# A gate on GpSimd's first casting DMAs, moved from x row tile 0 to x row tile 3, in a fused matmul, GELU, matmul kernel

## The chip, the cores and the metric

The kernel runs on one core of a Trainium2 chip. The metric is the device time of one execution in microseconds (us). A kernel's number is the median of several executions, and it is compared with runs of the kernel before made on the same chip in the same session. Sessions fell on different chips, so each has its own runs of the kernel before. Matmul and weight load are called PE and PEld in the profile, VectorE is DVE, ScalarE is ACT, GpSimd is POOL, SyncE is SP.

## The reference

```python
batch, m, k, h, n = 16, 512, 768, 3072, 768      # all fp32

def reference(x, w1, b1, w2):
    y = np.matmul(x, w1) + b1
    y = 0.5 * y * (1.0 + erf(y / np.sqrt(2.0)))
    return np.matmul(y, w2).astype(np.float32)
```

## The kernel before

The kernel computes in f16 and handles x in blocks of 1024 rows. Both matmuls are done by Strassen-like sums. Only the first few microseconds matter here. Two ways of loading stand side by side in them: SyncE's plain DMAs bring four x row tiles (128 rows each) and the first block of w1 as fp32, which VectorE casts; GpSimd's DMAs bring everything else and cast on the way.

```python
        for t in range(4):                                   # x row tiles 0 to 3, fp32
            nc.sync.dma_start(out=xf[:, t, :], in_=xr[:, t, :])
        wts[0] = slots[0]
        for half in range(2):                                # w1 block 0, two halves, fp32
            r = slice(half * KQ, (half + 1) * KQ)
            nc.sync.dma_start(out=wf[:, r, :], in_=w1r[:, r, 0:2 * P])
        # ... bias, zeros, identities ...
        nc.gpsimd.tensor_copy(out=xh_of(0, 4)[:, 0:1], in_=xf[:, 0, 0:1])   # the gate
        load_wt(1)                                           # casting DMA: w1 block 1
        for t in range(4, 8):
            load_x(0, t)                                     # casting DMAs: x row tiles 4 to 7
        for n in range(2, 4):
            load_wt(n)
        # ...
        spin(9)                                              # matmuls on zeros
        for t in range(4):
            xhs[t] = xh_of(0, t)
            nc.vector.tensor_copy(out=xhs[t], in_=xf[:, t, :])
            transpose_pe(0, t, copy_halves if t == 3 else nc.scalar.copy)
            # ...
            spin(2)
        # ... VectorE casts w1 block 0; matmuls of block 0 on the top rows ...
        plain(1, 0, 0, 0)                                    # w1 block 1 is needed here
        transpose_pe(0, 4)                                   # x row tile 4
        plain(1, 0, 0, 1)
        plain_done(1, 0, 0)
        transpose_pe(0, 5, nc.vector.tensor_copy)
        plain(1, 0, 1, 0)
        transpose_pe(0, 6)
        # ...
```

The gate copies one element of each of 128 rows. Its result is overwritten by the DMA of tile 4. It is there only because GpSimd runs in order: all its DMAs wait until the element that is read has landed.

Of the kernel before, what the change touches and what calls it, by code (L numbers as in the profile page):

```python
# [22 lines left out]
def kernel(  # L23
# [8 lines left out]
    nc = tc.nc  # L32
# [56 lines left out]
    def cut(off, n, pattern=None, **dims):  # L89
        ap = arena[:, off:off + n]  # L90
        return ap.rearrange(pattern, **dims) if pattern else ap
# [113 lines left out]
    with tc.manual_schedule():  # L205
# [27 lines left out]
        def load_wt(n):  # L233
            hi = hi_of(n)
            if n >= NH:
                sb, k = divmod(n, NH)
                wts[n] = wt_far[k - 4] if 4 <= k < 7 else wt_late[(sb + 2 + k - 7 * (k > 6)) % 4]
                nc.sync.dma_start(out=wts[n], in_=w1s[hi][:])
                return
            wts[n] = slots[n]  # L240
            nc.gpsimd.dma_start(out=w1_raw(wts[n]), in_=w1r[:, :, 2 * hi * P:2 * (hi + 1) * P])
# [70 lines left out]
        def xh_of(sb, t):  # L312
            if sb < ONE:
                return cut(sb * GR + GR // 2 + t * K, K)
            return xh_mid[t % 5 if t < 5 else t - 5] if sb == ONE else xh_late[t % 3]
# [423 lines left out]
        xf = cut(GR, 8 * K).bitcast(FP32).rearrange("p (t k) -> p t k", t=4)  # L739
# [13 lines left out]
        nc.scalar.activation(out=zero[:, 1, 0:1], in_=zero[:, 0, 0:1], func=GELU)  # L753
        make_identity(nc, ident[:])
        make_identity(nc, idf)
        nc.gpsimd.tensor_copy(out=xh_of(0, 4)[:, 0:1], in_=xf[:, 0, 0:1])
        load_wt(1)
        for t in range(4, 8):
            load_x(0, t)
# [420 lines left out]
```

## Time and profile before

| | |
|---|---|
| median of three runs | 851.17 us (851.04 to 851.5) |
| span of the profiled run | 848.7 us |
| TensorE busy | 843.3 us, 99% |
| first real matmul | 9.39 us |
| w1 block 1, x tiles 4, 5, 6 and 7 land | 11.65, 12.60, 13.57, 14.53 and 15.46 us |

The rows that carry the argument are in the prediction. One thing to know for reading them: a DMA row of GpSimd is the time that it spends on issuing the DMA (called descriptor writing here); the data moves later, on q0 (issued at 4.57, first packet at 8.60). The landing is taken from the view of each issue, which gives the time from issue to landing.

### The profile page before, as it was taken

To read this page: it belongs to the slowest core of one execution; us is meant where nothing else is said; L and a number is where in the kernel's file an instruction comes from. 1 tells how busy PE (TensorE), PEld (TensorE's weight loads), DVE (VectorE), ACT (ScalarE), POOL (GpSimd) and SP (SyncE) were. 2 spreads that over 40 slices of the span, in tenths; PEclk is the share of its full clock that TensorE was granted. 3 is DMA by queue.
4 is the path that set the end of the run, shared out by engine and by line. 5 is a ranking of instruction groups with operands and counts; after the bars stand their busy time and mean duration, and the time that the engine had idled before them with its cause. 6 is when DMAs were issued, how large, how long until landed. Compare 5 with 4: busy or idle time off the path is not lost.

```text
span 848.7 us, 16767 instructions
## 1 busy us (share of the span) xinstructions
PE 843.3 (99%) x6546; PEld 577.6 (68%) x6546; DVE 673.5 (79%) x1134; ACT 426.4 (50%) x700; POOL 94.9 (11%) x151
## 2 busy tenths in 40 slices
PE   9999999999999999999999999999999999999998
PEld 5444445796544897449964499545995469964798
DVE  5766679777857997679967799668996699957997
ACT  4777763231287413773247721587116761277611
POOL 5021100042200002000020000200002100010000
PEclk9999999999999999999999999999999999999999
DMA  9998796699998699987999489994999949984397
GB/s 228 216 274 166 166 221 232 233 201 221 361 329 206 207 341 370 255 201 259 335 368 300 118 296 346 359 276 123 319 356 335 281 114 324 369 300 168 106 308 282
DMA packets 144819, 222.11 MB, mean 262 GB/s; under 512 B 61964, under 2 KB 85444, under 8 KB 144740
## 3 DMA queue, kind: packets, MB, share of 16 engines
q1 hardware_dynamic: 117392, 178.85, 66.4%
q0 software_dynamic: 27168, 42.08, 22.4%
q8 instruction: 51, 0.84, 0.4%
q14 instruction: 28, 0.23, 0.1%
q10 hardware_dynamic: 180, 0.11, 0.0%
HBM read 181.78 MB, written 49.45 MB: 272 GB/s over the span
## 4 chain that ended last, share of the span: by engine, by line
PE 99%; DMA 1%; SPq 0%; DVE 0%; ACT 0%; issue 0%
PE bY L416 22%; PE bY L520 15%; PE bX L416 14%; PE bX L520 10%; PE bZ L416 7%; PE bW L416 7%; PE bZ L520 5%; PE bW L520 5%; PE bY L459 4%; PE bZ L459 2%; PE bW L459 2%; PE bY L608 2%; PE bX L608 1%; PE bX L459 1%; DMA arena<-in_x_dram 1%; PE bZ L608 1%
## 5 line engine op out<-in xcount | busy, mean ns | idle before, releaser
L210 DVE TENSOR_TENSOR arena<-arena 128x1536 f16<-128x1536 f16 (+6 forms) x638 | 409.8, 674 | 4.8 <-DMA arena<-arena 0.7
L416 PEld LDWEIGHTS <-arena 128*128 128x128 f16 x2016 | 196.6, 98 | 220.1 <-issue 0.5
L520 PEld LDWEIGHTS <-arena 128*128 128x128 f16 x3528 | 292.1, 98 | 8.2
L416 PE MATMUL bY<-arena 128*128 128x512 f16 (+1 forms) x864 | 214.5, 375 | 0.0
L639 DVE TENSOR_TENSOR arena<-bY,arena 128x512 f32<-128x512 f32 (+1 forms) x102 | 69.4, 680 | 118.2 <-PE bY L416 88.3
L632 ACT COPY bY<-bX 128x512 f32<-128x512 f32 (+1 forms) x145 | 79.6, 549 | 118.1 <-DVE arena L569 87.8
L520 PE MATMUL bY<-arena 128*128 128x192 f16 x1500 | 138.3, 246 | 0.0
L416 PE MATMUL bX<-arena 128*128 128x512 f16 (+1 forms) x576 | 138.3, 375 | 0.0
L432 ACT ACTIVATE arena<-arena,b1t 128x1024 f16<-128x1024 f32 x94 | 108.0, 1149 | 51.6 <-DVE arena L667 51.6
L652 ACT COPY arena<-bW 128x512 f32<-128x512 f32 (+1 forms) x149 | 81.9, 550 | 93.1 <-PE bW L520 43.9
L520 PE MATMUL bX<-arena 128*128 128x192 f16 x1020 | 93.1, 246 | 0.0
L667 DVE TENSOR_TENSOR arena<-bZ,arena 128x512 f32<-128x512 f32 (+1 forms) x102 | 69.2, 679 | 22.3 <-PE bZ L416 19.1
L416 PE MATMUL bZ<-arena 128*128 128x512 f16 (+1 forms) x288 | 76.2, 375 | 0.0
L416 PE MATMUL bW<-arena 128*128 128x512 f16 (+1 forms) x288 | 76.2, 375 | 0.0
L552 POOL DMA_DIRECT2D out_dram<-arena x42 | 30.5, 728 | 403.1 <-DVE arena L663 367.5
L683 ACT COPY bZ<-bY 128x512 f32<-128x512 f32 (+1 forms) x60 | 31.8, 529 | 80.8 <-PE bY L459 30.0
L437 ACT ACTIVATE arena<-bX,b1t 128x512 f16<-128x512 f32 x94 | 64.0, 681 | 9.8 <-PE bX L416 9.7
L437 ACT ACTIVATE arena<-bY,b1t 128x512 f16<-128x512 f32 x94 | 63.3, 674 | 0.0
L459 PEld LDWEIGHTS <-arena 128*128 128x128 f16 x432 | 42.2, 98 | 28.0 <-issue 0.2
L319 POOL DMA_DIRECT2D arena<-in_x_dram x60 | 33.7, 635 | 161.7 <-DMA arena<-arena 153.4
L520 PE MATMUL bZ<-arena 128*128 128x192 f16 x504 | 48.4, 246 | 0.0
L520 PE MATMUL bW<-arena 128*128 128x192 f16 x504 | 48.4, 246 | 0.0
(63 smaller groups left out, 426.8 us busy)
## 6 DMA issues: line engine op xcount, KB each, us to landing
arena<-w2s SPq DMA_DIRECT2D x299, 288.0 KB, 4.8
arena<-w1s SPq DMA_DIRECT2D x72, 672.0 KB, 7.0
out_dram<-arena POOLq DMA_DIRECT2D x46, 384.0 KB, 7.1
w2s<-arena SPq DMA_DIRECT2D x49, 288.0 KB, 4.5
arena<-in_x_dram POOLq DMA_DIRECT2D x60, 192.0 KB, 7.6
w1s<-arena SPq DMA_DIRECT2D x12, 672.0 KB, 5.9
arena<-in_w_dram POOLq DMA_DIRECT2D x17, 384.0 KB, 8.6
out_dram<-arena SPq DMA_DIRECT2D x13, 384.0 KB, 2.5
```

The source lines that it names most:

```text
L210: nc.vector.tensor_tensor(out=o, in0=a, in1=b, op=op)
L319: nc.gpsimd.dma_start(out=xhs[t], in_=xr[:, sb * 8 + t, :])
L416: nc.tensor.matmul(out=dst[:, r:r + w], lhsT=w1_op(self.wt, slot)[:, c, :], rhs=a[:, c, r:r + w], start=first and c == 0 and r == 0, stop= ...
L432: nc.scalar.activation(out=self.G[1][:, hi, :, :], in_=self.tmp, func=GELU, bias=b1t[:, 2 * hi + 1:2 * hi + 2])
L437: nc.scalar.activation(out=self.G[0][:, hi, row, :], in_=bank[:, 0:RH], func=GELU, bias=b1t[:, 2 * hi:2 * hi + 1])
L459: nc.tensor.matmul(out=dst[:, 0:N2], lhsT=a, rhs=w[:, :, c, :], start=first and c == 0, stop=c == self.C - 1, skip_group_check=True)
L520: nc.tensor.matmul(out=dst[:, t * N4:(t + 1) * N4], lhsT=a, rhs=w[:, c, :], start=first and c == 0 and t == ts[0], stop=c == NQ - 1, skip_ ...
L608: nc.tensor.matmul(out=dst[:, t * N4:(t + 1) * N4], lhsT=a, rhs=self.w[q][:, c, :], start=first and c == 0 and t == 0, stop=c == NQ - 1, s ...
L632: nc.scalar.copy(out=bY[u.g % 2][:, 0:u.F], in_=bX[u.g % 2][:, 0:u.F])
L639: nc.vector.tensor_tensor(out=u.c22(), in0=bY[u.g % 2][:, 0:u.F], in1=w[:, 0:u.F], op=ADD)
L652: nc.scalar.copy(out=w[:, 0:u.F], in_=bW[:, 0:u.F])
L667: nc.vector.tensor_tensor(out=u.c12(), in0=bZ[:, 0:u.F], in1=w[:, 0:u.F], op=ADD)
```

## The change

The intent, as far as the edit tells it, is to keep GpSimd's loads out of the way until SyncE's four x tiles, on which the first matmul waits, are all there.

```diff
-        nc.gpsimd.tensor_copy(out=xh_of(0, 4)[:, 0:1], in_=xf[:, 0, 0:1])
+        nc.gpsimd.tensor_copy(out=xh_of(0, 4)[:, 0:1], in_=xf[:, 3, 0:1])
         load_wt(1)
```

## The prediction

> **What bounds the kernel now.** I read the page first: its busy table, then the chain of work that ended last.
>
> ```profile
> span 848.7 us, 16767 instructions
> PE 843.3 (99%) x6546; PEld 577.6 (68%) x6546; DVE 673.5 (79%) x1134; ACT 426.4 (50%) x700; POOL 94.9 (11%) x151
> PE 99%; DMA 1%; SPq 0%; DVE 0%; ACT 0%; issue 0%
> ```
>
> The chain is TensorE for 99% of the span. So GpSimd, which the change touches, matters in one way only: by what it makes TensorE wait for. A microsecond in which TensorE stands still is not won back, because nothing later on the chain is idle to absorb it. The chain's 1% of DMA lies in the first ten microseconds, so I then read the chain in order of time in the window 0 to 9.5 us (start, length, what):
>
> ```profile
> 2.14 5.54 DMA arena<-in_x_dram
> 7.70 0.57 DVE arena L772
> 8.32 0.52 PE bT L333 x6
> 8.87 0.49 ACT arena L329
> 9.39 0.38 PE bX L788
> ```
>
> The first real matmul, at 9.39, hangs on x row tile 3: issued on SyncE's queue at 2.14, landed at 2.14 + 5.54 = 7.68, cast on VectorE, transposed on TensorE, copied on ScalarE. Before it TensorE only spins on zeros.
>
> From 9.39 TensorE works without a hole. The timeline shows where GpSimd's loads meet it: GpSimd's rows, then weight loads (start, length, engine, line, operation, and in brackets the idle time before and what ended it):
>
> ```profile
> 4.06 0.57 POOL L756 CAST arena<-arena 128x1 f16<-128x1 f32 x1 [2.25 <-DMA arena<-in_x_dram]
> 4.57 0.97 POOL L241 DMA_DIRECT2D arena<-in_w_dram  x1
> 5.53 2.34 POOL L319 DMA_DIRECT2D arena<-in_x_dram  x4
> ...
> 12.10 0.31 PEld L788 LDWEIGHTS <-arena 128*128 128x128 f16 x2
> 12.71 0.36 PEld L333 LDWEIGHTS <-arena 128*128 128x128 f16 x6 [0.29 <-issue]
> 13.62 0.43 PEld L333 LDWEIGHTS <-arena 128*128 128x128 f16 x6 [0.22 <-DMA arena<-in_x_dram]
> 14.57 0.46 PEld L333 LDWEIGHTS <-arena 128*128 128x128 f16 x6 [0.20 <-DMA arena<-in_x_dram]
> ```
>
> The one-element cast at 4.06 is the gate that the change moves: it waits for x tile 0 and the casting DMAs stand behind it in GpSimd's order. They are one block of w1 (384 KB), x tiles 4 to 7 (192 KB each), then more blocks of w1. By the view of each issue (start plus time to landing) the w1 block lands at 4.57 + 7.08 = 11.65 and x tiles 4, 5, 6 at 12.60, 13.57, 14.53. TensorE first uses that block at 12.10 and transposes tiles 4, 5, 6 with weight loads at 12.71, 13.62, 14.57. For tiles 5 and 6 that is 0.05 and 0.04 us after the landing, and the row names the DMA as the releaser. So this stretch is fed just in time: **the casting loads have almost no slack**.
>
> The DMA queue view says why they land so late. In the window 0 to 8.55 us:
>
> ```profile
> q1 hardware_dynamic: 1212, 2.21, 76.5%
> q10 hardware_dynamic: 36, 0.01, 0.5%
> ```
>
> There is no line for q0, GpSimd's queue. Although issued from 4.57, its first packet starts at 8.60; until then all the transfer goes to q1, SyncE's four x tiles and two halves of w1 block 0. q0 follows when q1 runs dry, and the two share only 8.6 to 9.6 us (in that window q0 has 0.12 MB, q1 0.14 MB). From 9.6 to 12 us q0 alone moves a mean of 205 GB/s and is backlogged.
>
> **What the Trainium skill says.** "DMA: Bandwidth & Descriptors", section "Queues, rings and completion order", says that each DMA engine takes turns among the queue rows that have work, a packet at a time, and its section "Issuing engines are not separate DMA queues" that all queues run on the same 16 engines and interleave. By that alone the early q0 loads would rob x tile 3 of bandwidth, and the change would help. The trace agrees for 8.6 to 9.6 us and disagrees before: no q0 packet in four microseconds after the issue. The trace decides.
> The same page, "Anatomy of one DMA — SWDGE (gpsimd) path", gives a fixed cost of some 2.0 us for a DMA from GpSimd, mostly completion. This trace has about 2.9 us, worked out below.
> "TensorE: Matmul & The Clock Gate", Part 1, says that the array falls back to half clock after an idle window of about 3.4 us. The stall that I expect is shorter; the granted clock of before is 1.00 in every 2 us window that I read.
>
> **The change part by part.** No instruction is added, removed or reordered (the comparison of instruction order finds one difference, the wait of the cast at L756: another DMA's semaphore). Only time moves.
>
> 1. The gate. Before, tile 0 landed at 4.00, the cast began at 4.06 and the first DMA was issued at 4.57, 0.57 after the landing. With tile 3 at 7.68 the issue comes at 7.68 + 0.57 = 8.25, so 3.68 us later.
> 2. What of it was hidden. Of the 3.68 us the old issue spent most waiting behind q1: issue to first packet took 8.60 - 4.57 = 4.03 us. Where q0 had been idle and q1 was not holding it up, issue to first packet took 1.52, 1.55 and 1.58 us (issues at 50.35, 77.54 and 101.50). So the first packet of the changed kernel should start at 8.25 + 1.55 = 9.80, against 8.60: **1.20 us later**.
> 3. Landing. The two unhindered single w1 blocks (384 KB, at 50.35 and 77.54) landed 4.8 us after issue; a 960 KB load (at 101.50) took 7.6. The difference, 590 KB (in thousands) in 2.8 us, is 210 GB/s, the rate above; so a 384 KB load is 1.9 us of moving plus 2.9 us fixed. That puts the w1 block at 8.25 + 4.8 = 13.05, 1.40 us later than 11.65. The route through the first packet gives 1.2. I take **1.3 us**, and the same for x tiles 4 to 7, which follow at the pace of the queue (0.96 us each, as before): about 13.9, 14.9, 15.8 for tiles 4, 5, 6.
> 4. What TensorE loses. Matmuls on w1 block 1 began at 12.10 against a landing of 11.65 and some 0.15 us from landing to first product: 0.3 us of slack, so they are about 1.0 late. Tile 4's transposes began at 12.74 against 12.60 landed: no slack beyond the 0.15. They are 1.3 late, and tiles 5 and 6 follow at the same distance. The stall is 1.3 us in all: the first part before the w1 matmuls, the rest before tile 4.
> 5. What comes back. Without q0 in 8.6 to 9.6 us, the second half of w1 block 0 lands earlier than 9.87 by up to 0.4 us (0.14 MB of q1 at some 365 GB/s takes 0.4 us). That moves VectorE's third cast by 0.1 us at most, since the second one ran until 9.78, and TensorE isn't waiting there: I count 0. x tile 3 itself gains nothing, as no q0 packet ran before it landed.
> 6. Later loads. The other w1 blocks and x tiles of the next row block come out of the same backlogged queue and shift by the same 1.3 us, but so does TensorE. In the waits of 28 to 80 us only one wait of VectorE for a transposing DMA shows (0.7 us), and none of TensorE. I count 0.
>
> Sum: +1.3 us. 851.17 + 1.3 = **852.5 us**, 0.15%.
>
> **The rivals.**
> (a) The intended gain: SyncE's first tiles land sooner, and the start comes forward. Tiles 0 to 3 land at 4.00, 4.96, 6.64, 7.68, and the pace dips between 5 and 6 us (264 KB against 356 the microsecond before), when GpSimd is writing descriptors. Were that dip GpSimd's doing, tile 3 could come 0.3 to 0.5 us sooner, and the gate with it: the loss would shrink to about 0.8, hence 852.0. Against it: no packet of q0 is there, and the pace is back above 360 while GpSimd still issues.
> (b) The load is hidden anyway, as 4.03 us of queueing were mostly idle: change 0, 851.2. Against it: the 1.2 us of step 2 remain, and the weight loads follow the landings by 0.05 us.
> (c) Descriptor writing, now at 8.25 to some 14 us, collides with VectorE's casts of w1 block 0 and the first sums. Before, the cast at 4.98 took 0.92 against 0.56 for its equals while GpSimd issued, and the third cast of w1 took 0.84. It could add 0.3 us to a start that is just in time; but these casts overlapped with issues before as well. With it, 852.8.
> (d) TensorE's gap lowers its clock: a 3.4 us window at half clock would cost 1.7 us more, 854. I give it under 2%.
>
> **Range and chances.** The delay of the landings lies between 0.9 (the unhindered figures being pessimistic, some of the sharing saved) and 1.5; with (c) up to 1.8. The three runs of before spread over 0.46 us. So 851.8 to 853.2. A change of 2% would be 17 us, and the whole part of the program that the gate touches is 4 us long: within 2% is all but certain.
>
> **What would show it.** In the changed profile: the cast at L756 at about 7.7, the first GpSimd DMA at 8.2, the first q0 packet near 9.8, x tile 3 landing at 7.7 and the first real matmul at 9.4 as before, TensorE idle about 1 us just before 13 and a little before 14, weight loads at L333 released by the DMA, then the same spacing to the end. It is wrong if tile 3 lands clearly before 7.5, if the w1 block lands before 12.3, or if the gap is made good before 60 us.

## The result, and the profile after

The changed kernel took 853.37 us (median of 6, 852.8 to 854.3), the one before 851.34 (6 runs, 851.04 to 851.8): 2.03 us more. The ratio is 1.0025, with a 95% interval of 1.0012 to 1.0038. A ratio is the mean time of one kernel's fast runs over that of the other's of the same rounds, so it is not quite the ratio of the medians. It is a clear small loss, and larger than the predicted 1.3 us and just above the range's upper end of 853.2.

The page of the changed kernel, the lines that answer to those shown of before:

```profile
span 851.0 us, 16767 instructions
PE 843.5 (99%) x6546; PEld 577.3 (68%) x6546; DVE 673.1 (79%) x1134; ACT 426.7 (50%) x700; POOL 94.9 (11%) x151
PE 98%; DMA 1%; POOL 0%; SPq 0%; DVE 0%; issue 0%
```

TensorE's busy time is what it was (843.5 against 843.3). The span grew by 2.3 us, nearly all of it waiting, and GpSimd has appeared on the chain. The chain of waits of the changed kernel, in order of time from 7 to 20 us (start, length, what):

```profile
2.14 5.47 DMA arena<-in_x_dram
7.61 0.05 issue
7.66 0.57 POOL arena L756
8.24 0.91 POOL arena L241
9.15 0.55 POOL arena L319
9.70 6.28 DMA arena<-in_x_dram
15.98 0.04 issue
16.02 0.51 PE bT L333 x6
```

Before, the chain went from the landing of x tile 3 by its cast, transposes and copy to the first matmul at 9.39. Now it goes from the same landing (7.61) to the gate, to GpSimd's first two issues, and to a DMA of 6.28 us: x tile **5**, issued at 9.70 and landed at 15.98. The stretch 9.39 to 16.02, in which TensorE worked without a hole before, is no longer on the chain at all.

GpSimd's rows of the changed kernel, then its weight loads, as shown of before:

```profile
7.66 0.57 POOL L756 CAST arena<-arena 128x1 f16<-128x1 f32 x1 [5.85 <-DMA arena<-in_x_dram]
8.18 0.97 POOL L241 DMA_DIRECT2D arena<-in_w_dram  x1
9.14 2.38 POOL L319 DMA_DIRECT2D arena<-in_x_dram  x4
...
13.05 0.33 PEld L788 LDWEIGHTS <-arena 128*128 128x128 f16 x3 [1.35 <-DMA arena<-in_w_dram]
14.09 0.35 PEld L333 LDWEIGHTS <-arena 128*128 128x128 f16 x6 [0.71 <-issue]
14.39 0.37 PEld L788 LDWEIGHTS <-arena 128*128 128x128 f16 x3
16.02 0.34 PEld L333 LDWEIGHTS <-arena 128*128 128x128 f16 x6 [1.25 <-DMA arena<-in_x_dram]
```

The three weight loads that wait are for w1 block 1 (12.10 before), x tile 4 (12.71 before) and x tile 5 (13.62 before). The delay grows at each: 0.95, 1.38, 2.40 us (2.29 for the transposes of tile 5 themselves, which began at 13.73 before). TensorE's own rows of the timeline give its idle time at the same three places:

```profile
13.05 0.82 PE L788 MATMUL bX<-arena 128*128 128x512 f16 x3 [0.86 <-DMA arena<-in_w_dram]
14.12 0.50 PE L333 MATMUL bT<-ident,arena 128*128 128x128 f16 x6 [0.24 <-DMA arena<-in_x_dram]
16.02 0.51 PE L333 MATMUL bT<-ident,arena 128*128 128x128 f16 x6 [0.76 <-DMA arena<-in_x_dram]
```

The landings, by the view of each issue, are 13.01 for the w1 block (13.05 was worked out), 13.98 for tile 4 (13.9), but 15.98 for tile 5 (14.9). From tile 4 to tile 5 passed 2.00 us; before it was 0.97, and tiles 6 and 7 followed tile 5 by 0.96 and 0.92 again. So there is one hole of about 1 us in the stream, and it is the part that the prediction did not have.

The view of stretches of one microsecond shows it. Its columns are the stretch and its length, then the busy us (and the number of instructions) of PE, PEld, DVE, ACT and POOL, then the granted clock, the DMA share and the GB/s moved. First the kernel before:

```profile
12.00:13.00 1.00, 1.00 (x10) 0.49 (x8) 0.90 (x3) 0.98 (x2) 0.61 (x2) 1.00 1.15 206
13.00:14.00 1.00, 1.00 (x13) 0.64 (x11) 0.00 (x0) 0.72 (x2) 0.57 (x2) 1.00 1.15 206
14.00:15.00 1.00, 1.00 (x14) 0.64 (x11) 0.56 (x1) 0.67 (x2) 0.57 (x2) 1.00 1.20 199
```

Then the changed kernel, the same view:

```profile
10.00:11.00 1.00, 1.00 (x7) 0.44 (x5) 0.93 (x3) 0.00 (x0) 1.00 (x3) 1.00 0.98 107
12.00:13.00 1.00, 0.20 (x1) 0.00 (x0) 0.00 (x0) 0.92 (x2) 1.00 (x2) 1.00 1.33 207
13.00:14.00 1.00, 0.82 (x3) 0.21 (x3) 0.90 (x3) 0.00 (x0) 1.00 (x3) 1.00 1.16 135
14.00:15.00 1.00, 0.88 (x9) 0.56 (x9) 0.17 (x1) 0.35 (x1) 1.00 (x2) 1.00 0.94 160
```

In the changed kernel the queue gets going slowly (107 GB/s in 10 to 11), reaches the usual 207, and falls to 135 and 160 in 13 to 15 us, while the engines count as busy: their packets take longer. The trace's record of DMA packets, which the views don't print, says by how much. A q0 packet of 512 bytes takes 60 ns and one of 1536 bytes 135 ns. Up to 17.5 us the kernel before has no q0 packet over 300 ns; the changed one has 23, up to 1154 ns, in two clusters: 9.9 to 10.4, just after its first packet at 9.84, and 12.8 to 14.6, with one more at 15.5.

**The trace of before shows the same slow stretches later on.** After 20 us it has 268 such packets. Its queue starts anew at 51.87, on a load issued at 50.35, and SyncE's queue moves next to nothing until 62 (0.01 MB). Four stretches of the same view:

```profile
52.00:53.00 1.00, 1.00 (x6) 0.48 (x5) 0.00 (x0) 1.00 (x2) 0.00 (x0) 1.00 1.11 116
55.00:56.00 1.00, 1.00 (x7) 0.46 (x5) 0.90 (x2) 0.66 (x1) 1.00 (x2) 1.00 1.16 210
56.00:57.00 1.00, 1.00 (x6) 0.42 (x5) 0.93 (x4) 1.00 (x3) 0.42 (x1) 1.00 0.77 98
60.00:61.00 1.00, 1.00 (x6) 0.49 (x5) 0.65 (x1) 1.00 (x2) 0.96 (x2) 1.00 1.01 109
```

A slow start, the usual pace, a second slow stretch from about 56.4 (when, by the bytes moved, the queue comes to the load issued at 54.88), and a third from 59 to 62 with 37 long packets. Two loads of 384 KB land 1.87 us apart (55.16 and 57.03), the next 4.36 us later (61.39). TensorE is busy all the while, so it costs nothing there. Five more traces were looked at in this place (d_before_again, the changed kernel, a_gate1, b_before_hold, d_bridge3): all fall from over 200 GB/s to 71 to 140 there. So the effect is not made by the change; the change moved the queue's first start into it, at a place where TensorE waits.

### The profile page after: what moved, and what is told of

The parts are those of the page before. It is cut to its first block, busy times and chain, and to the rows that moved or that the text cites. A ratio compares the mean times of both kernels' runs of the same rounds, so it can differ in the third digit from the quotient of the medians.

```text
span 851.0 us, 16767 instructions
## 1 busy us (share of the span) xinstructions
PE 843.5 (99%) x6546; PEld 577.3 (68%) x6546; DVE 673.1 (79%) x1134; ACT 426.7 (50%) x700; POOL 94.9 (11%) x151
## 4 chain that ended last, share of the span: by engine, by line
PE 98%; DMA 1%; POOL 0%; SPq 0%; DVE 0%; issue 0%
PE bY L416 21%; PE bY L520 15%; PE bX L416 14%; PE bX L520 10%; PE bZ L416 7%; PE bW L416 7%; PE bZ L520 5%; PE bW L520 5%; PE bY L459 4%; PE bZ L459 2%; PE bW L459 2%; PE bY L608 2%; DMA arena<-in_x_dram 1%; PE bX L608 1%; PE bX L459 1%; PE bZ L608 1%
```

## The experiments

Two questions are separate. Why is the queue late at all (the 1.3 us foreseen)? And where does the hole come from (the other 1 us)? For the second I took three theories to the chip: **descriptor writing** (GpSimd's next issues, at 11.5 to 14 us, disturb the transfer), **cold restart** (the DMA engines stood idle between SyncE's last and GpSimd's first packet), and **chance**. A fourth, **fresh descriptors** (the queue runs badly when it comes to descriptors that GpSimd has only just written), came up on the way.

This table sums up the traces. "First issue" and "first q0" are GpSimd's first DMA issue and the first packet of its queue; "age" is the second less the first; "long" is the number of q0 packets over 300 ns before 17.5 us; "steps" are the times from one landing to the next, from w1 block 1 to tile 4, 4 to 5, 5 to 6 and 6 to 7. All in us. "Ratio" is to the kernel before of the same session, with its 95% interval; 0.001 is 0.85 us.

| run | first issue | first q0 | age | long | w1 block lands | steps | ratio |
|---|---|---|---|---|---|---|---|
| before | 4.57 | 8.60 | 4.03 | 0 | 11.65 | 0.95, 0.97, 0.96, 0.93 | 1 |
| d_before_again | 4.60 | 8.52 | 3.92 | 0 | 12.04 | 0.98, 0.94, 0.96, 0.93 | one run |
| changed | 8.18 | 9.84 | 1.67 | 23 | 13.01 | 0.97, 2.00, 0.96, 0.92 | 1.0025 (1.0012 to 1.0038) |
| a_again | 8.31 | 9.98 | 1.67 | 19 | 13.15 | 0.95, 2.17, 0.89, 0.96 | 1.0023 (1.0010 to 1.0035) |
| d_after_third | 8.75 | 10.42 | 1.67 | 8 | 13.72 | 0.96, 1.84, 0.97, 0.93 | one run |
| a_gate1 | 5.84 | 8.42 | 2.58 | 0 | 11.63 | 0.94, 0.96, 0.95, 0.96 | 1.0001 (0.9988 to 1.0013) |
| d_gate1_again | 5.76 | 8.52 | 2.75 | 0 | 11.98 | 0.95, 0.95, 0.98, 0.93 | one run |
| c_gate2_again | 6.84 | 8.76 | 1.92 | 13 | 12.26 | 0.95, 1.27, 1.02, 1.12 | 1.0004 (0.9988 to 1.0019) |
| a_gate2 | 7.53 | 9.22 | 1.69 | 10 | 12.79 | 0.97, 1.20, 0.95, 1.07 | 1.0030 (1.0016 to 1.0044) |
| b_gate_w | 9.63 | 11.36 | 1.73 | 9 | 14.62 | 0.95, 1.21, 0.97, 0.93 | 1.0032 (1.0019 to 1.0044) |
| a_no_gate | 1.76 | 5.87 | 4.10 | 1 | 12.50 | 1.22, 0.97, 0.94, 0.95 | 1.0044 (1.0031 to 1.0058) |
| b_hold | 9.25 | 10.92 | 1.67 | 9 | 14.15 | 0.95, 1.30, 1.08, 1.00 | 1.0023 (1.0009 to 1.0037) |
| b_before_hold | 4.37 | 8.68 | 4.31 | 0 | 11.85 | 0.95, 0.95, 0.95, 0.96 | 0.9993 (0.9980 to 1.0005) |
| b_bridge | 8.23 | 9.90 | 1.67 | 16 | 14.73 | 1.00, 0.91, 0.95, 0.95 | 1.0035 (1.0023 to 1.0048) |
| d_bridge3 | 8.51 | 11.42 | 2.92 | 0 | 14.82 | 0.95, 0.95, 0.99, 0.91 | 1.0039 (1.0023 to 1.0056) |
| c_split3 | 4.48 | 8.54 | 4.06 | 25 | 12.22 | 1.33, 0.95, 1.38, 1.03 | 1.0011 (0.9998 to 1.0023) |
| c_split_w | 4.46 | 8.77 | 4.31 | 23 | 12.02 | 2.53, 1.21, 0.99, 1.12 | 1.0035 (1.0022 to 1.0047) |

All runs gave the right result. One thing blurs single traces: the landing of x tile 3 itself varies from execution to execution, from 7.6 to 8.7 us, and not only where the edit could be the cause (8.07 in the second trace of the kernel before). A trace's delay against another trace therefore has half a microsecond of its own.

A second thing blurs the medians. In three traces (a_no_gate, b_gate_w, d_bridge3) TensorE's clock falls to a half for 3.41 us after an idle stretch, which by estimate costs up to 1.7 us (half of 3.41) and lowers a run's mean clock by 0.002. The runs with a mean granted clock of 0.998 or less are two of five of a_no_gate (856.41 and 856.93), three of five of b_bridge (855.04 to 855.47), all four of d_bridge3, and one each of b_gate_w (855.42), a_gate2 (854.56) and c_split_w (856.49); none of the kernel before and none of the changed kernel. In those runs the loss is probably in part the clock's, and not the queue's.

### Is it chance? The changed kernel and the kernel before again

No edit. a_again and d_after_third are the changed kernel, d_before_again the one before.

> The changed kernel once more, for a second trace. Seen in its first trace: the w1 block landed at 13.01, x tile 4 at 13.98, but x tile 5 only at 15.98 (2.00 us after tile 4, where before took 0.97), and the run was about 2.0 us slower than before. Theory 'cold restart' (the casting queue starts on idle DMA engines, and stalled packets come with such a start and again some 3 us later): tile 5 is late again, gap from tile 4 to tile 5 of 1.5 to 2.2 us, and 1.7 to 2.3 us slower than before. Theory 'chance' (the hole of 1 us is an accident of that execution): gap 1.0 us, shift of TensorE 1.3 to 1.4 us, and the median about 1.4 us slower than before.

> The changed kernel, unchanged, for a third trace: w1 block at 13.0 to 13.6, tile 4 0.96 later, tile 5 1.3 to 2.2 later than tile 4, stalled packets at the start of q0 and 3 us after. If the hole were an accident of the two traces so far: tile 5 1.0 later.

> The kernel before, unchanged, for a second trace: no q0 packet over 300 ns before 20 us, tiles 4 to 7 land 0.95 to 1.0 us apart, x tile 3 between 7.6 and 8.3.

a_again: 853.25 us against 851.33, 1.92 more. Tile 5 came 2.00, 2.17 and 1.84 us after tile 4 in the three traces of the changed kernel, 0.97 and 0.94 in the two of before. It is not chance. TensorE's idle time in the three places is 1.87, 2.03 and 1.84 us in the three traces (0.86 + 0.24 + 0.76 in the first), which is about the loss in the medians.

### How the loss grows with the gate: tile 1, tile 2, w1 block 0, no gate

```diff
-        nc.gpsimd.tensor_copy(out=xh_of(0, 4)[:, 0:1], in_=xf[:, 0, 0:1])
+        nc.gpsimd.tensor_copy(out=xh_of(0, 4)[:, 0:1], in_=xf[:, 1, 0:1])   # a_gate1, d_gate1_again
+        nc.gpsimd.tensor_copy(out=xh_of(0, 4)[:, 0:1], in_=xf[:, 2, 0:1])   # a_gate2, c_gate2_again
+        nc.gpsimd.tensor_copy(out=xh_of(0, 4)[:, 0:1], in_=wf[:, 0, 0:1])   # b_gate_w
+                                                                            # a_no_gate: the line taken out
```

> Gate on x row tile 1 (lands 4.98). First GpSimd DMA at 5.5, descriptors ready about 7.0, still before SyncE's queue runs dry at about 8.6. All theories that put the loss in the first packet after SyncE's queue has drained expect the landings of before (w1 block 11.65, x tile 4 12.60) and no change: within 0.3 us of before. A theory that each microsecond of later issue costs something expects 1/3.6 of the loss, about +0.6 us.

> Gate on tile 1 again. Its descriptors were 2.6 us old at the first packet (8.42). 'Fresh' theory with a limit near 2 us: clean again, landings as before. If tile 1's own landing varies enough to bring the age under 2 us, stalled packets.

> Gate on x row tile 2 (lands 6.5). First GpSimd DMA at about 7.1, first packet not before 8.65 by the 1.55 us of an unhindered start: just at the end of SyncE's queue. Queue theory: w1 block lands within 0.3 us of 11.65, no cold start, within 0.4 us of before. Proportional theory: 2.5/3.6 of the loss, +1.4 us.

> Gate on tile 2 once more: its profile was of its fastest run (852.5) and its other runs went up to 854.6, so it cost as much as the gate on tile 3 although its first issue came 0.65 us sooner. If the cost follows from when tile 2 lands (6.2 to 7.6 in the traces so far) against SyncE's queue running dry, the profile with a landing of about 6.3 has its first packet by 8.7, no stalled packets and is at before's level, one with a landing of 7 or more has them and is 1.5 to 2.5 us slower.

> Gate on the first half of w1 block 0 (lands 8.7 to 8.8) in place of x tile 3: 1.1 us later than the changed kernel. First issue at 9.35, first packet at about 10.9, on DMA engines idle for 1.4 us. Both theories: w1 block lands at about 14.15, x tile 4 at 15.1, TensorE another 1.1 us late and the same hole: 3.0 to 3.5 us slower than before. If the changed kernel's loss were not set by the first packet but by the gate's distance from tile 0 in proportion, +2.6.

> No gate: GpSimd issues its casting DMAs at about 1.8. If its packets interleave with SyncE's from the start, x row tile 3 lands 1 to 3 us later than 7.7 and the first real matmul comes that much after 9.4: +1 to +3 us. If GpSimd's packets wait behind SyncE's whatever the issue (as between 4.6 and 8.6 in before), nothing changes: within 0.3 us.

**Tile 1** costs nothing: issued 1.27 us later than before, the first packet came at 8.42 all the same, the w1 block landed at 11.63 (11.65 before), TensorE has no hole, and the time is the same (851.52 against 851.33). Later issue as such costs nothing here. It is the trace that speaks against the proportional theory: the interval of the ratio, -1.0 to +1.1 us, leaves room for its +0.6. **Tile 2** is on the edge: its own landing varies, the first packet came at 8.76 or 9.22, and the loss was within the noise on one chip (852.24 against 851.44) and as large as the changed kernel's on another (853.86 against 851.33). Neither theory of a_gate2 foresaw 2.5 us. Only its fastest run was profiled, so what its slower runs did is open. The expectation of c_gate2_again was missed too: tile 2 landed at 6.28, for which no long packets were foreseen, and there were 13. **The first half of w1 block 0** gave 854.17 against 851.59, 2.6 more: below the 3.0 to 3.5 expected, and the number that the proportional theory gave. The hole was smaller (1.21), the first part larger as expected (TensorE idle 1.93 us before the w1 matmuls), and in its trace, that of the slowest of its five runs, TensorE's clock fell as well.

**No gate** is the worst of these, 854.81 against 851.33, more than the 1 to 3 us expected, and it shows what the gate is for. Tile 3 landed only 0.8 us later (8.47), but the first real matmul began at 11.28, and TensorE then waited 1.99 us more for the second half of w1 block 0. Its packets did not wait for SyncE's queue to run dry: from 5.9 us both queues moved side by side (in 6 to 8.5 us q0 0.15 MB and q1 0.51 MB), and the second half of w1 block 0 landed at 14.09 in place of 9.87. So my picture "q0 waits until q1 is dry" was too simple. What fits all traces is order of issue: SyncE's last load is issued at 3.1 to 3.6 us; a GpSimd load issued after that, at 4.4 to 6.8, gets its first packets at 8.4 to 8.8, when SyncE's last load is being moved; one issued at 1.76, before SyncE's last three, moves beside them. **The gate has done its work once it holds GpSimd back past SyncE's last issue, and tile 0 at 4.0 us already does that.** No run issues between 1.8 and 4.4 us, so that the last issue is the exact limit is inferred. Tile 3 protects nothing more.

### Descriptor writing: held back in the changed kernel, moved into the transfer in the kernel before

```diff
@@ b_hold, on the changed kernel
+        nc.gpsimd.tensor_copy(out=slots[2][:, 0:1], in_=xh_of(0, 4)[:, 0:1])
         for n in range(2, 4):
             load_wt(n)
@@ b_before_hold, on the kernel before
+        nc.gpsimd.tensor_copy(out=slots[2][:, 0:1], in_=wf[:, KQ, 0:1])
         for n in range(2, 4):
             load_wt(n)
```

> The changed kernel, with GpSimd's next descriptor writing (the three w1 blocks of 0.84 us each, at 11.5 to 14.0 in the changed kernel) held behind a one-element copy that waits for x tile 4 (lands about 14.0). Theory 'descriptor writing' (GpSimd's writing of descriptors beside the x tiles makes the hole): x tile 5 lands 1.0 us after tile 4 instead of 2.0 to 2.2, and the kernel is about 1.0 us faster than the changed one, 1.3 slower than before. Theory 'cold restart': the hole stays, 1.8 to 2.2 us between the tiles, total 1.8 to 2.6 slower than before.

> The kernel before, with GpSimd's three w1 issues (7.86 to 10.36 in before) held until w1 block 0 has landed (9.87), so that they run at about 10.4 to 12.9, beside x tiles 4 and 5, as in the changed kernel, while the queue itself takes over from SyncE's without a lull. Theory 'descriptor writing': a hole appears, x tile 5 about 2 us after tile 4, about +1 us. Theory 'cold restart': no hole, 0.95 to 1.1 us between them, within 0.3 us of before.

b_before_hold is the clean one. GpSimd wrote its three descriptor sets from 10.99 to 13.5 and four more after that, beside tiles 4 to 6, as in the changed kernel; GpSimd's rows of its timeline are:

```profile
10.99 2.48 POOL L241 DMA_DIRECT2D arena<-in_w_dram  x3 [0.30 <-POOL arena L760]
13.44 2.18 POOL L319 DMA_DIRECT2D arena<-in_x_dram  x4
```

and its stretches, with the columns as above:

```profile
12.00:13.00 1.00, 1.00 (x7) 0.39 (x6) 0.93 (x3) 1.00 (x2) 1.00 (x2) 1.00 1.15 206
13.00:14.00 1.00, 1.00 (x12) 0.64 (x11) 0.02 (x1) 0.66 (x2) 1.00 (x3) 1.00 1.17 209
```

GpSimd is busy for the whole of both microseconds and the queue moves 206 and 209 GB/s, as without it. No long packet, steps of 0.95, 850.89 us against 851.59. Descriptor writing beside the transfer does not make the hole. In b_hold the hole shrank (1.30) but did not close, and the time was 853.86 against 851.59, no better than the changed kernel; b_gate_w, which did not hold anything back, has the same smaller hole. The theory is refuted.

### An idle queue: SyncE kept busy between the two

```diff
@@ on the changed kernel, after the loop that casts tiles 0 to 3
+        nc.sync.dma_start(out=xf[:, 0, :], in_=xr[:, 0, :])                 # b_bridge
+        for t in range(3):                                                  # d_bridge3
+            nc.sync.dma_start(out=xf[:, t, :], in_=xr[:, t, :])
```

These reload a tile into its own place, where nobody reads it again; they add bytes, so they are not meant to be fast.

> The changed kernel, with one more load of 384 KB on SyncE's queue behind the w1 halves (x row tile 0 again, into its own place, read by nobody), so that the DMA engines do not stand idle between SyncE's last load and GpSimd's first packet (in the changed kernel a lull from about 9.1 to 10.6). Theory 'cold restart': the casting queue takes over at full speed as in before; x tile 5 lands 1.0 us after tile 4; w1 block within 0.5 us of 13.0; about 1.0 us faster than the changed kernel. Theory 'descriptor writing' or 'bandwidth alone': the hole stays at 2.0 us and the landings come up to 1 us later still, as 384 KB more has to move: 2 to 3 us slower than before.

> The changed kernel with three more loads of 384 KB on SyncE's queue (x row tiles 0 to 2 again, into their own places), issued before GpSimd's, so that SyncE's queue runs dry only at about 12.5, when GpSimd's descriptors (issued from 8.2) are over 3 us old. Theory 'fresh descriptors': the casting queue starts clean, no q0 packet over 300 ns, x tile 5 lands 0.95 to 1.1 us after tile 4 and tile 6 as much later; the total is 3.5 to 5 us slower than before, as 1.2 MB more has to move. Theory 'the later start as such' (any start after about 9 brings stalled packets some 3 us later): q0 packets over 300 ns some 3 us after its start, one step between tiles of 1.2 us or more.

b_bridge brought SyncE's last packet from 9.3 to 10.32, past GpSimd's first at 9.90: no idle stretch (in the changed kernel it was 9.31 to 9.84). Still 16 long packets, at 10.0 to 11.4 and 13.1 to 14.1 us. The hole between tiles 4 and 5 was gone (0.91), but the second cluster fell on the w1 block and tile 4 instead, and the block landed at 14.73, 1.7 later than without the bridge. The total, 855.04 against 851.59, is 3.4 us more in the medians and 3.0 by the ratio, at or above the upper end of the 2 to 3 of the rivals; but the median run has a mean clock of 0.998, and the two runs at full clock are 1.9 and 2.2 us above before. So the total decides nothing, and the packets must. By them idle engines are not the condition, and the hole does not belong to tile 5: it comes some 3 us after the queue's start, and falls on what is then moving.

d_bridge3 has the same gate and about the same issue times, but SyncE's queue ran to 12.5, and GpSimd's first packet came 2.92 us after its issue. No long packet at all, and steps of 0.95, 0.95, 0.99 and 0.91. Its stretches:

```profile
13.00:14.00 1.00, 0.00 (x0) 0.00 (x0) 0.00 (x0) 0.25 (x1) 1.00 (x2) 1.00 1.42 204
14.00:15.00 1.00, 0.14 (x1) 0.13 (x2) 0.16 (x1) 0.00 (x0) 0.33 (x1) 0.77 1.20 210
15.00:16.00 1.00, 1.00 (x3) 0.26 (x2) 0.91 (x3) 0.00 (x0) 0.56 (x1) 0.50 1.13 203
```

The queue moves over 200 GB/s at the very time at which the changed kernel has its hole. (TensorE idles 2.3 us for the extra megabyte, and 854.82 against 851.45 is the price, with a clock at half for 3.41 us in it; the total was expected to be 3.5 to 5 more and is 3.4.) That is what "fresh descriptors" foresaw and "a later start brings long packets" did not.

### Half of the change: only the x tiles held back

```diff
@@ on the kernel before
         load_wt(1)
+        nc.gpsimd.tensor_copy(out=xh_of(0, 4)[:, 0:1], in_=xf[:, 3, 0:1])    # c_split3
+        nc.gpsimd.tensor_copy(out=xh_of(0, 4)[:, 0:1], in_=wf[:, KQ, 0:1])   # c_split_w
         for t in range(4, 8):
```

> Part of the change alone: GpSimd's first DMA (w1 block 1) keeps the gate on x row tile 0, only the DMAs behind it (x tiles 4 to 7 and what follows) are held until tile 3 has landed. Theory 'no lull' (what costs is that the casting queue has nothing ready when SyncE's queue runs dry, and then starts with stalled packets): the first packet comes at 8.6 as in before, the next descriptors are ready at about 9.8, before the w1 block has moved (10.9), so x tile 4 lands at 12.6, tile 5 1.0 us later, no packets over 300 ns, and the time is within 0.3 us of before. Theory 'a later gate costs what it is late' (3.7 us later issues): most of the 2.0 us stay.

> As the split before, but the second gate on the second half of w1 block 0 (lands 9.9): x tiles are issued from 10.5, their first packet is due at 12.0, while the w1 block is through at 10.9. Theory 'no lull': the w1 block lands at 11.65 as in before, then the lull puts tile 4 at about 14.1 (1.5 later than 12.60), with stalled packets at the start and tile 4 to 5 or 5 to 6 over 1.1 us: 1.5 to 2.2 us slower than before. Theory 'only the first DMA matters': within 0.3 us of before.

c_split3 missed its expectation of "within 0.3 us, no long packets": 852.57 against 851.44, about half of the loss (the interval of the ratio just includes no change), and 25 long packets at 10.5 to 16.2 us. The w1 block started clean at 8.54, and there was no lull, but the queue came to tile 4's packets 1.35 us after their issue. This is what ended "cold restart" and suggested the age of the descriptors. c_split_w, with a real lull (11.71 to 12.42 us), put tile 4 at 14.55 and cost 2.7 us (854.17 against 851.44), more than the 1.5 to 2.2 expected: there the first issue of GpSimd was on time, and it helped nothing.

### What the runs say together

Sorted by age, the traces in which the queue starts on one block of issues fall apart cleanly: with 2.58 us or more between the first issue and the first packet (six traces: before twice, gate 1 twice, before_hold, bridge3) there is no packet over 300 ns (the longest has 291); with 1.92 us or less (eight traces) there are 8 to 23. The two splits have their second block used at 1.35 and 1.27 us and have 25 and 23. No gate, at 4.10, has one, with both queues running. c_gate2_again and a_gate1 differ in hardly anything but the age: both start 0.9 us before SyncE's last packet. Two rivals can be set aside from the traces at hand. The number of loads queued at the start grows with the age too, but in c_split_w the w1 block was alone in the queue, 4.31 us old at its first packet, and none of its packets took over 60 ns. And VectorE's work beside GpSimd's descriptor writing is not the condition: in the kernel before the queue started at 8.60 in the midst of both (casts from 8.81, issues from 7.86) without a long packet.

The rule is a description of the first 17.5 us of these traces. Age is not separated from having had to wait: wherever the packets came 1.3 to 1.9 us after the issue, GpSimd's queue began about as soon as it could, and wherever it was clean SyncE's queue had held it up. Later in the traces the rule is no more than a tendency: in the kernel before, the starts at 51.87, 87.62 and 103.09 (ages 1.52, 1.44 and 1.58) have 3, 11 and 17 long packets in their first microsecond, that at 79.10 (1.55) has one; but d_bridge3 has a start at 356.95 with 20, on a load that was 3.9 us old. Why a queue that starts on descriptors just written runs slowly at first, and above all why it stalls again 3 us later (after the start at 51.87 it did not: no long packet from 53 to 56), is not shown by any run and **stays open**.

## Why the prediction was right or wrong

| step of the prediction | predicted | measured |
|---|---|---|
| 1 gate and first issue | 8.25 | 8.18 |
| 2 first q0 packet | 9.80, 1.20 later | 9.84, 1.24 later |
| 3 w1 block lands | 13.05 (1.3 taken as the shift) | 13.01, 1.36 later |
| 3 tile 4 | 13.9 | 13.98 |
| 3 tile 5 | 14.9 | **15.98** |
| 4 w1 matmuls late by | 1.0 | 0.95 |
| 4 tile 4's transposes late by | 1.3 | 1.38 |
| 4 tile 5's transposes late by | 1.3 | **2.29** |
| 5 x tile 3, first matmul | 7.7, 9.4 | 7.61, 9.43 |
| sum | +1.3 | +2.03 in the medians, +2.3 in the trace |

**The direction and the mechanism were right.** TensorE is fed just in time there, the gate's delay is mostly hidden behind SyncE's queue, the rest reaches TensorE undiminished, and nothing later absorbs it.

**The step that failed is step 3, its second half:** "the same for x tiles 4 to 7, which follow at the pace of the queue (0.96 us each, as before)". The pace was read off a queue whose descriptors were 4 us old. Starting on fresh ones, the queue lost another 1.03, 1.20 and 0.87 us between tiles 4 and 5 in three traces of three (2.00, 2.17, 1.84 less the 0.97 of before). Step 4 inherited it: "tiles 5 and 6 follow at the same distance". With that term the sum of the first trace is 1.38 + 0.91 = 2.29 (the extra 0.91 is how much later still tile 5's transposes started).

Step 3 mixed two states of the queue. Its first half took 1.55 and 4.8 us from the starts at 50.35 and 77.54, which were on fresh descriptors like the changed kernel's, and so had the slow start in them: 13.05 against 13.01. Its second half took the pace from the old queue at 12 to 15 us. The prediction's own trace had the other pace as well, in the view of 52 to 62 us shown above; that view was not asked for. A little luck was in the first packet: 0.12 us more from issue to packet than assumed (1.67 against 1.55) nearly cancelled a tile 3 that landed 0.07 sooner.

**A reading that was wrong without harm:** that q0 "follows when q1 runs dry". Without the gate the two moved side by side. The order of issue decides, and in both kernels all of SyncE's loads are issued first.

**The rivals.** (a) is refuted: with GpSimd silent until 7.66, the dip between 5 and 6 us is still there (234 KB against 264), and tile 3 landed at 7.61 against 7.68. Why the stream dips there is open. (b) is refuted for tile 3 and true for tile 1. (c) had the wrong sign: VectorE's three casts of w1 block 0 took 1.58 us in a row in place of 1.92, and its first sum began at 10.37 in place of 10.77; GpSimd was issuing beside them in both kernels, so what sped them up isn't shown. TensorE did not wait there, so this won nothing, as step 5 says. (d) did not happen in the changed kernel (granted clock 1.00 in each stretch shown), but it did in three experiments, and after shorter idle stretches than the 3.4 us that the prediction leaned on (1.93 us in b_gate_w): that the clock held here was not shown to be safe.

## What to carry to other kernels

A gate that keeps one DMA queue out of another's way needs, as far as these runs tell, to outlast the other's last *issue*, not its last landing; holding it longer only uses up the hidden time. Before delaying an issue, compare the time from issue to first packet with and without a queue in front: as long as the queue in front is clearly longer, the delay is free (here with 2.58 us from issue to first packet; with 1.92 the long packets were there already), and what goes beyond it is lost in full if the consumer works just in time. A pace read off a running queue does not hold for one that has just been started: count an extra loss for the start, and look for it a few microseconds later as well. Look in the trace at hand for a place where the queue starts in the same way, and read the pace there; the kernel before had one at 51.87.

## What the Trainium skill lacked or had wrong

- "DMA: Bandwidth & Descriptors" ("Queues, rings and completion order", "Issuing engines are not separate DMA queues"): it describes turn-taking between queues with work. The runs show it for a load issued before the other queue's last three (q0 and q1 side by side from 5.9 us in a_no_gate), but a load issued after them had no packet for 4.03 us. The page doesn't tell that what is already queued is served ahead, as these runs suggest.
- The same page, "Anatomy of one DMA — SWDGE (gpsimd) path": a fixed cost of about 2.0 us; here a 384 KB casting load took 4.83 us, of which 1.9 are moving (0.39 MB at 205 GB/s), so 2.9. Nor is it mostly completion: the load issued at 77.54 in the kernel before took 1.55 us to its first packet, 2.96 for its packets, and 0.28 from the last packet's end to the landing.
- I found no page that tells of a queue running slowly on descriptors just written, and stalling again some 3 us on: 8 to 23 packets of up to 1292 ns in place of 60 to 135, in the changed kernel 0.9 to 1.2 us lost between two landings.
- "TensorE: Matmul & The Clock Gate", Part 1: half clock "after ≥1 idle window (~3.4µs)". The length agrees (3.41 us at half clock in b_gate_w), but the idle time that brought it on was shorter: 1.93 us in one piece in b_gate_w, 1.99 (after one of 1.23) in a_no_gate, 2.34 in d_bridge3. In the 3.41 us before the fall TensorE had still been busy for 1.26, 1.42 and 1.40 us. In b_bridge 2.53 us of idling did not bring it on. Three products of 512 columns take 0.81 us at full clock; in a_no_gate, the timeline's row of TensorE reads

```profile
15.55 1.48 PE L787 MATMUL bY<-arena 128*128 128x512 f16 x3
```

and in b_gate_w

```profile
16.18 1.49 PE L788 MATMUL bX<-arena 128*128 128x512 f16 x3
```
